# Three edits to a hybrid decoder layer kernel: a wider group of down tiles at a block's end, the order of the GLU's columns, and an early product taken from x without its 1/rms

## The chip, the cores and the metric

One core of a Trainium2 chip runs the whole layer as one program. The metric is the device time of one execution in microseconds (us). TensorE (PE, with its weight loads as PEld), VectorE (DVE), ScalarE (ACT), GpSimd (POOL) and SyncE (SP, which issues most DMAs) each work through a queue of their own, in order, and wait for each other by semaphores.

## The reference, cut to what matters

`norm(a)` is a / rms(a) times a gain; L = 2064 positions (16 meta tokens and 2048 tokens), 1024 features, 2816 hidden features in the MLP.

```python
h = concat(meta, x)                                   # 2064 x 1024
hn = norm(h)
b_gate, c_gate, v, u = split(hn @ w_in, 4)            # 512 columns each
conv_out = b_gate * causal_dwconv(c_gate * v)         # width 3
y = s5_scan(u) + d * u                                # 32 groups, 64 complex states each
g = gelu(y)
ssm_out = g * sigmoid(g @ w_glu)                      # the half-GLU, 512 x 512
h = h + concat(norm(conv_out), norm(ssm_out)) @ w_out
hn = norm(h)
up = causal_dwconv(hn @ w_up) + bias                  # 2 x 2816 columns
h = h + (silu(up[:, :2816]) * up[:, 2816:]) @ w_down
out = norm(h)[16:]
```

## The kernel before, in words

**Numbers.** Everything is float32. A product is made of two fp32r parts of each operand: a high part (`h_..`, `wh_..`, `ah`) that ACT rounds (L248) and a low part (`l_..`, `wl_..`, `al`) that DVE subtracts (L109). Three matmuls stand for one: high by high (L138), low by high (L139), high by low (L142). Features lie on the 128 partitions in k tiles, positions along the free axis.

**Positions.** The 2064 positions are cut into six pieces q of 344, and two pieces make one of three blocks b of 688 (in the MLP the first block has 672 and the others 688). A feature tile in PSUM or SBUF that holds a block has 128 x 688 elements, and one matmul takes 344 of them (336 in the first MLP block).

**Part one, projections.** `u_block(b)` (L877) makes the 512 columns of u of a block in four units of 8 k tiles x 2 pieces x 3 matmuls, and `conv_block(b)` (L896) the twelve units of v, c_gate and b_gate. The order written out is: u of block 0, conv of block 0, u of block 2 (early, L987), u of block 1, conv of block 1, conv of block 2. In the trace x of piece q is `x_c`, its scaled form `t_c`, its parts `h_c` and `l_c`, and the names in the program carry q: c4 and c5 are the two pieces of block 2. The 1/rms of a piece is made by squares (`sq_c`, L164), sums (DVE), a product with ones on PE (`st_c`, L188), a small scaling (`sv_c`), a power on POOL (L199), a diagonal (`dg_c`, L203), a product that spreads it (`sb_c`, L208), and a copy (`rs_c`, L213). For block 0, `raw_x` (L378) splits x times the gain straight into parts (ACT L389, DVE L390), and the 1/rms, kept in one buffer for two pieces (`rs0`, L373), is multiplied into what PE gives (`ut`, `vs`, `tc`, `tp`). For all other pieces `prep_x` (L348) multiplies the 1/rms into x first (`t_c`, 8 instructions at L241) and splits that; so c4 and c5 are scaled for the early u, and later loaded and scaled again for the conv of block 2. The steps of such preparations are generators that are stepped between the units (`after_unit`, L856); `late` holds last halves back until a unit has taken its place.

**Part two, GLU and output projection.** gelu(y) comes back from memory as `gt`, with 8 interleaved rows j of 258 columns per feature tile, so that position = 8 c + j. `prep_glu` (L1016) splits it (`gh` on ACT, `gl` on DVE) into position order: it reads rows j one after another in runs of 43 and writes with a step of 8 elements (`tokens`, L1007). `glu_block` (L1072) makes the product `pg`, the sigmoid `sg`, and multiplies it into `gt` in place. `prep_ssm` (L1026) squares `gt` (`sq_ms`), scales it (`t_ms`, contiguous) and splits it into position order (`h_ms`, `l_ms`). `mc` names the same steps for the conv half.

**Part three, MLP.** For each block, `up` (L1457) makes pairs of up tiles (`xy`, `z`), the conv and SiLU, and the split result `ah`, `al`; the 22 hidden tiles are in chunks of 4, 4, 4, 3, 3 and 4. `down` (L1499) multiplies a chunk into the 8 output tiles m. A list of groups of m says how many output tiles are open together: in a group every tile does all k but the chunk's last first, and then all do the last k, which is the one that is ready last. Before the last chunk a group holds two tiles (`first_pair`, L1535), at the end of blocks 0 and 1 three (L1555: the third in two tiles of the `z` pool). In the last block the end is done by pieces c of 344 with first_pair for c = 0. Each finished tile is copied by ACT (`ev`, L1525 or L1528, three buffers) and added to `h_d` in memory by a DMA of POOL (L1529); in the last block DVE adds it to `acc` instead. PSUM has two `xy` buffers, two `z` buffers and two `aux` buffers here. `Feed` (L1234) loads and splits the weights in order.

The order within each queue is made by a scheduler when the program is built, by its own estimates, under the dependences; so an edit can shift instructions that it does not name.

Of the kernel before, what the change touches and what calls it, by code (L numbers as in the profile page):

```python
# [11 lines left out]
F32 = mybir.dt.float32  # L12
# [45 lines left out]
def layer_kernel(ctx, tc, xq, pk, w_in, w_glu, w_out, w_up, w_down, ssm_s, ssm_m, y):  # L58
# [52 lines left out]
    def mul(out, a, b):  # L111
        tt(out, a, b, ALU.mult)
# [260 lines left out]
    def rs_tile(name):  # L373
        return cp.tile([P, 2, QM], F32, tag="rsk", bufs=1, name=name)

    rs0 = rs_tile("rs0")[:, :, :QL]

    def raw_x(q, res):  # L378


        xs, out = [], []
        for i in range(2):
            xs += load_halves((xq[q, :, 4 * i : 4 * i + 4, :],), QL, f"c{q}{i}")
            yield
        for i, x in enumerate(xs):
            hi, lo = hl_tile(QL, f"h_c{q}_{i}"), hl_tile(QL, f"l_c{q}_{i}")
            for k in range(4):
                g = col(C_MIX + 4 * i + k)
                S.activation(hi[:, k, :], x[:, k, :], AF.Copy, scale=g)  # L389
                V.scalar_tensor_tensor(  # L390
                    out=lo[:, k, :], in0=x[:, k, :], scalar=g, in1=f32(hi[:, k, :]), op0=ALU.mult, op1=ALU.subtract
                )
            out.append((hi, lo))
            yield
        res.append(out)
        yield from inv_rms(xs, QL, f"c{q}", rs0[:, q, :])


    sgn = col(C_SGN)
# [456 lines left out]
    def after_unit(n=1, n_prep=1):  # L856
        if a1 is None:
            ssm.step(4)
            if not ssm.q:
                start_a1()  # L860
                prep.add(prep_x(4, hu, other=True), prep_x(5, hu, late=late))
        else:
            ssm.step(n)
            prep.step(n_prep)
# [12 lines left out]
    def u_block(b, hs, last=False):  # L877
        rhs = rhs_of(hs)
        for m in range(4):
            if last and m == 3:  # L880
                while len(late) < 2:
                    prep.step()
            ps = unit(rhs, f"pu_{b}_{m}", m == 0 or last and m == 3)
            ut = cvp.tile([P, NJ, 86], F32, tag="ut", bufs=2, name=f"ut_{b}_{m}")
            if last and m == 3:
                take_late(2)
            by_j = lambda a: a.rearrange("p c (x j) -> p c x j", j=NJ)
            out = ut.rearrange("p j (c x) -> p c x j", c=2)
            if b == 0:
                mul(out, by_j(ps[:, :, :QL]), by_j(rs0))  # L890
            else:
                S.activation(out, by_j(ps[:, :, :QL]), AF.Copy)
            dma(out=u_d[:, m, :, b * 86 : b * 86 + 86].rearrange("j p c -> p j c"), in_=ut)
            after_unit(n_prep=5 if last else 1)

    def conv_block(b, hs, late_after=False, n_prep=1):  # L896
        rhs = rhs_of(hs)

        for j in range(4):
            pv_ = unit(rhs, f"cv_{b}_{j}", False)  # L900
            vs = cvp.tile([P, B2], F32, tag="cs", bufs=3, name=f"vs_{b}_{j}")
            if b == 0:
                mul(two(vs), pv_[:, :, :QL], rs0)
            else:
                S.activation(two(vs), pv_[:, :, :QL], AF.Copy)
            after_unit(n_prep=n_prep)
            pc = unit(rhs, f"cc_{b}_{j}", False)
            cv = cvp.tile([P, B2 + 2], F32, tag="cvt", bufs=1, name=f"cvt_{b}_{j}")
            V.tensor_copy(cv[:, 0:2], halo[:, j, :])
            if b == 0:  # L910
                mul(two(vs), two(vs), rs0)
            tt(two(cv[:, 2:]), pc[:, :, :QL], two(vs), ALU.mult)
            V.tensor_copy(halo[:, j, :], cv[:, B2 : B2 + 2])
            tp = cvp.tile([P, B2], F32, tag="cs", bufs=3, name=f"tc_{b}_{j}")
            S.activation(tp, cv[:, 2:], AF.Copy, scale=col(C_CW + 8 + j))
            axpy(tp, cv[:, 1 : B2 + 1], col(C_CW + 4 + j), tp)
            axpy(tp, cv[:, 0:B2], col(C_CW + j), tp)
            if b == 0:
                mul(two(tp), two(tp), rs0)
            after_unit(n_prep=n_prep)  # L920
            if late_after and j == 3:
                while len(late) < 2:
                    prep.step()
            pb = unit(rhs, f"cb_{b}_{j}", j == 3)
# [42 lines left out]

    hc = [[] for _ in range(3)]
    hu, late = [], []
    first = [raw_x(q, hc[0]) for q in range(2)]  # L970
    next(first[0])
    stream.raw.append(load_weights(*stream.items.popleft()))
    next(first[0])
# [42 lines left out]
    def prep_glu(b, res, **kw):  # L1016
        for c in range(2):
            hi, lo = hl_tile(QL, f"gh_{b}_{c}", **kw), hl_tile(QL, f"gl_{b}_{c}", **kw)
            c0 = (2 * b + c) * 43
            src = gt[:, :, :, c0 : c0 + 43]  # L1020
            S.activation(tokens(hi), src, AF.Copy)
            tt(tokens(lo), src, f32(tokens(hi)), ALU.subtract)
            res.append(((hi, lo),))
            yield

# [46 lines left out]
    def glu_block(b):  # L1072
        until(hg[b])
        rhs = rhs_of(hg[b])
        for m in range(4):
            ps = mm_tile(f"pg_{b}_{m}")
            product([ps[:, c, :QL] for c in range(2)], stream.take(), rhs, 4, by_chunk=m == 0)
            sg = ev_tile(f"sg_{b}_{m}")
            S.activation(two(sg), ps[:, :, :QL], AF.Sigmoid)
# [334 lines left out]
    for b in range(3):  # L1414
# [84 lines left out]
        def down(ci, ms, cs=(0, 1), into=None):  # L1499
# [51 lines left out]
        if b < 2:  # L1551
            while "scaled" not in hf[b + 1]:
                prep.step()
            hf[b + 1]["go"] = True
            for ms in [(0, 1, 2)] + [(m,) for m in range(3, KD)]:  # L1555
                down(last, ms)
                prep.step(len(ms))
            prep.drain()
# [3 lines left out]
        else:  # L1562
# [109 lines left out]
```

## Time and profile before

| | |
|---|---|
| time of three runs | 2195.51, 2195.66 and 2199.68 us, median 2195.66 us |
| the profiled execution | 2199.4 us, its span 2197.6 us |
| TensorE clock granted over the span | 0.984 of full speed |
| instructions in the span | 33162 |

The profiled execution took 2199.4 us, with 1.8 us of it outside the span. Rows of a timeline give start, duration, engine, line, operation, output <- inputs, tile shapes and xcount, and in brackets the idle time of the engine before it and what ended it. Rows of groups give a count, the busy time and the mean ns of one instruction. Rows of windows give a stretch, its length, each engine's busy time, the granted TensorE clock (1.00 is full speed), the share of the DMA engines and GB/s. Rows of waits give an engine and line, what was waited for, the total in us, how often, and the longest.

### The profile page before, as it was taken

Reading aid. Unit: us, or ns where it says so; the run is one execution under the profiler, and the core shown is the slowest. Engines: PE = TensorE matmul, PEld = TensorE weight load, DVE = VectorE, ACT = ScalarE, POOL = GpSimd, SP = SyncE. Lnnn points to the kernel's source line nnn. Section 1 sums busy time; section 2 is a strip of 40 time slices with the busy share of each in tenths; the row PEclk is TensorE's granted clock in tenths of the full one; section 3 lists DMA queues with packets and bytes.
Section 4 is the critical chain, followed back from the end, with each engine's and each line's share of the span. In section 5 each row is a group of like instructions: output and inputs, shape, how many; then the busy total and the mean of one; then the engine's idle time right before and its main releaser. Section 6 shows DMA issues by size and latency. Waiting matters only on the chain.

```text
span 2197.6 us, 33162 instructions
## 1 busy us (share of the span) xinstructions
PE 2119.1 (96%) x13012; PEld 2057.7 (94%) x13012; DVE 1688.0 (77%) x2539; ACT 1097.5 (50%) x1651; POOL 153.2 (7%) x174
## 2 busy tenths in 40 slices
PE   8997999999899999999999999999999999999997
PEld 7997999998898999999999999999899999999996
DVE  8896498857866796886679878777768878767776
ACT  4135333236523365554556556555456556545555
POOL 0000000000000001101110010100111010110010
PEclk9998999999999999999999999999999999999999
DMA  7376544352475336635552554744554362654463
GB/s 246 104 219 169 142 144 146 116 169 74 144 232 187 100 98 158 157 90 122 133 127 76 144 119 122 184 103 130 147 136 109 103 166 82 163 118 99 98 168 118
DMA packets 170750, 300.29 MB, mean 137 GB/s; under 512 B 32416, under 2 KB 104800, under 8 KB 170464
## 3 DMA queue, kind: packets, MB, share of 16 engines
q1 hardware_dynamic: 149856, 246.41, 36.3%
q0 software_dynamic: 19584, 47.52, 13.0%
q10 hardware_dynamic: 1152, 4.23, 0.5%
q8 instruction: 102, 1.67, 0.3%
q14 instruction: 56, 0.46, 0.1%
HBM read 214.29 MB, written 83.82 MB: 136 GB/s over the span
## 4 chain that ended last, share of the span: by engine, by line
PE 60%; issue 8%; DVE 5%; ACT 3%; DMA 3%; POOL 1%; SPq 0%; POOLq 0%; DVEq 0%; ACTq 0%
PE xy L1427 9%; PE xy L1429 8%; PE xy L1428 8%; PE dn L138 6%; PE dn L139 6%; PE dn L142 6%; PE pz L1429 3%; PE pz L1427 3%; PE pz L1428 3%; PE po L138 2%; PE po L142 2%; PE po L139 1%; DMA v_b<-h_d 1%; DMA gt<-g_d 1%; ACT h_ms L1038 1%
## 5 line engine op out<-in xcount | busy, mean ns | idle before, releaser
L109 DVE TENSOR_TENSOR wl_up<-wr_up,wh_up 128x1024 fp32r<-128x1024 f32 x198 | 241.8, 1222 | 140.7 <-ACT wh_up L248 138.5
L138 PE MATMUL dn<-ah,wh_dn 128*128 128x344 f32 (+1 forms) x1024 | 327.8, 324 | 11.4 <-ACT ah L248 8.8
L139 PE MATMUL dn<-al,wh_dn 128*128 128x344 f32 (+1 forms) x1024 | 325.5, 321 | 0.4 <-DVE al L109 0.3
L248 ACT ACTIVATE wh_up<-wr_up 128x1024 fp32r<-128x1024 f32 x198 | 209.6, 1059 | 230.8 <-PE dn L139 56.4
L1427 PE MATMUL xy<-h_t,wh_up 128*128 128x344 f32 (+1 forms) x792 | 262.8, 332 | 0.0
L1429 PE MATMUL xy<-h_t,wl_up 128*128 128x344 f32 (+1 forms) x792 | 253.4, 320 | 0.0
L1428 PE MATMUL xy<-l_t,wh_up 128*128 128x344 f32 (+1 forms) x792 | 252.7, 319 | 0.0
L142 PE MATMUL dn<-ah,wl_dn 128*128 128x344 f32 (+1 forms) x1024 | 248.1, 321 | 0.0
L138 PEld LDWEIGHTS dn<-ah,wh_dn 128*128 128x128 f32 x1024 | 193.2, 189 | 17.1 <-ACT ah L248 9.7
L1529 POOL DMA_DIRECT2D h_d<-ev x136 | 118.3, 870 | 1261.8 <-ACT ev L1525 1251.4
L139 PEld LDWEIGHTS dn<-al,wh_dn 128*128 128x128 f32 x1024 | 194.2, 190 | 2.0 <-DVE al L109 1.2
L1427 PE MATMUL xy<-h_b,wh_up 128*128 128x344 f32 (+1 forms) x528 | 175.6, 334 | 6.1 <-ACT ev L1525 4.6
L142 PEld LDWEIGHTS dn<-ah,wl_dn 128*128 128x128 f32 x1024 | 178.4, 190 | 0.0
L1428 PE MATMUL xy<-l_b,wh_up 128*128 128x344 f32 (+1 forms) x528 | 169.0, 320 | 0.0
L1429 PE MATMUL xy<-h_b,wl_up 128*128 128x344 f32 (+1 forms) x528 | 167.6, 320 | 0.0
L1427 PEld LDWEIGHTS xy<-h_t,wh_up 128*128 128x128 f32 x792 | 149.2, 188 | 17.1 <-ACT z L1472 11.1
L248 ACT ACTIVATE wh_dn<-wr_dn 128x512 fp32r<-128x512 f32 (+1 forms) x144 | 85.5, 594 | 133.6 <-issue 56.7
L1428 PEld LDWEIGHTS xy<-l_t,wh_up 128*128 128x128 f32 x792 | 149.9, 189 | 0.0
L1429 PEld LDWEIGHTS xy<-h_t,wl_up 128*128 128x128 f32 x792 | 149.6, 189 | 0.0
L115 DVE SCALAR_TENSOR_TENSOR g<-z,pv,g 128x688 f32<-128x688 f32 (+1 forms) x132 | 122.3, 926 | 23.7 <-ACT g L1432 22.9
L115 DVE SCALAR_TENSOR_TENSOR v<-z,pneg,v 128x688 f32<-128x688 f32 (+1 forms) x132 | 122.4, 927 | 10.3 <-ACT v L1432 9.0
L109 DVE TENSOR_TENSOR wl_dn<-wr_dn,wh_dn 128x512 fp32r<-128x512 f32 (+1 forms) x144 | 92.3, 644 | 45.6 <-ACT wh_dn L248 44.9
(413 smaller groups left out, 5358.3 us busy)
## 6 DMA issues: line engine op xcount, KB each, us to landing
wr_up<-in_w_up SPq DMA_DIRECT2D x132, 512.0 KB, 5.0
h_d<-ev POOLq DMA_DIRECT2D x88, 344.0 KB, 6.6
wr_dn<-in_w_down SPq DMA_DIRECT2D x96, 256.0 KB, 2.6
wr_cw<-in_w_in SPq DMA_DIRECT2D x36, 512.0 KB, 4.6
h_d<-ev POOLq DMA_DIRECT2D x48, 336.0 KB, 6.7
x_c<-in_xq SPq DMA_DIRECT2D x16, 688.0 KB, 6.4
wr_dn<-in_w_down SPq DMA_DIRECT2D x48, 192.0 KB, 2.3
xr<-in_xq SPq DMA_DIRECT2D x24, 344.0 KB, 3.7
```

The costliest lines, as they stand in the source:

```text
L109: V.tensor_tensor(out, a, b, op=op)
L115: V.scalar_tensor_tensor(out=out, in0=a, scalar=s, in1=b, op0=ALU.mult, op1=ALU.add)
L138: T.matmul(ps[c], hi[:, k, :], xh, start=k == 0, stop=False)
L139: T.matmul(ps[c], hi[:, k, :], xl, start=False, stop=False)
L142: T.matmul(ps[c], lo[:, k, :], xh, start=False, stop=k == nk - 1)
L248: S.activation(hi, t, AF.Copy)
L1038: S.activation(tokens(hi), t, AF.Copy)
L1427: T.matmul(ps, hi[:, j, :], xh[:, j, :], start=start and j == 0, stop=False, **kw)
L1428: T.matmul(ps, hi[:, j, :], xl[:, j, :], start=False, stop=False, **kw)
L1429: T.matmul(ps, lo[:, j, :], xh[:, j, :], start=False, stop=j == 3, **kw)
L1529: G.dma_start(out=h_d[:, m, s0 : s0 + no], in_=ev, accum_op=ALU.add)
```

## The change

It has three parts, and each stands by itself.

1. **Down at a block's end.** In blocks 0 and 1 the first group of the last chunk holds four tiles in place of three, and the fourth lies in two `aux` tiles. In block 2 the first group of piece c = 0 holds four tiles in place of two; the third and fourth lie in the `z` pool.
2. **GLU.** `gh` and `gl` keep the order of `gt` (8 rows j of 43) instead of position order, so that input and output are read and written in runs of 43. The product is over features, so its columns come out in the same order; `sg` is then read contiguous, and `gt` times `sg` runs over 43 at a time.
3. **Early u of block 2.** x of c4 is loaded right after u of block 0, and c4 and c5 go through `raw_x` in the place of `prep_x`: their parts are made from x times the gain, and their 1/rms (`rs_2`, in the one buffer that `rs_0` had) is multiplied into `ut` by DVE where ACT copied it. The later pass over c4 and c5, for the conv of block 2, is as it was.

```diff
@@ raw_x
-    def raw_x(q, res):
+    def raw_x(q, res, b, other=False, late=None):
...
+        kw = dict(pool=xf2, tag="xhl2", bufs=4) if other else {}
...
-        for i, x in enumerate(xs):
-            hi, lo = hl_tile(QL, f"h_c{q}_{i}"), hl_tile(QL, f"l_c{q}_{i}")
+        def split_half(i, x):
+            hi, lo = hl_tile(QL, f"h_c{q}_{i}", **kw), hl_tile(QL, f"l_c{q}_{i}", **kw)
...
-        yield from inv_rms(xs, QL, f"c{q}", rs0[:, q, :])
+        for i, x in enumerate(xs):
+            if late is None:
+                split_half(i, x)
+            else:
+                late.append(lambda x=x, i=i: split_half(i, x))
+            yield
+        if b not in rs_of:
+            rs_of[b] = rs_tile(f"rs_{b}")[:, :, :QL]
+        yield from inv_rms(xs, QL, f"c{q}", rs_of[b][:, q % 2, :])
@@ after_unit
-                prep.add(prep_x(4, hu, other=True), prep_x(5, hu, late=late))
+                prep.add(ahead[0], raw_x(5, hu, 2, late=late))
@@ u_block
-            if b == 0:
-                mul(out, by_j(ps[:, :, :QL]), by_j(rs0))
+            if b in rs_of:
+                mul(out, by_j(ps[:, :, :QL]), by_j(rs_of[b]))
@@ after u_block(0, hc[0])
+    ahead = [raw_x(4, hu, 2, other=True)]
+    next(ahead[0])
+    next(ahead[0])
@@ prep_glu
-            S.activation(tokens(hi), src, AF.Copy)
-            tt(tokens(lo), src, f32(tokens(hi)), ALU.subtract)
+            hj, lj = (a.rearrange("p k (j c) -> p k j c", j=NJ) for a in (hi, lo))
+            S.activation(hj, src, AF.Copy)
+            tt(lj, src, f32(hj), ALU.subtract)
@@ glu_block
-            g = gt[:, m, :, b * 86 : b * 86 + 86]
-            mul(g, g, tokens(sg))
+            g = gt[:, m, :, b * 86 : b * 86 + 86].rearrange("p j (c x) -> p c j x", c=2)
+            mul(g, g, two(sg).rearrange("p c (j x) -> p c j x", j=NJ))
@@ down
+                elif i < 2 + 2 // len(cs):
+                    ps = [ps_z.tile([P, 512], F32, tag="z", name=f"{name}_{c}")[:, :nn] for c in cs]
                 else:
-                    ps = [ps_z.tile([P, 512], F32, tag="z", name=f"{name}_{c}")[:, :nn] for c in cs]
+                    ps = [aux_tile(f"{name}_{c}")[:, :nn] for c in cs]
@@ the ends of blocks 0 and 1
-            for ms in [(0, 1, 2)] + [(m,) for m in range(3, KD)]:
+            for ms in [(0, 1, 2, 3)] + [(m,) for m in range(4, KD)]:
@@ the end of block 2
-                for ms in first_pair if c == 0 else [(m,) for m in range(KD)]:
+                for ms in [(0, 1, 2, 3)] + [(m,) for m in range(4, KD)] if c == 0 else [(m,) for m in range(KD)]:
```

The program still has 12752 instructions of PE and 2541 of DVE; ACT has 1671 in place of 1661; POOL's order is the same.

**PE at the end of block 0.** In `dn_0_5_m` the m is the output tile, and the next number its piece; `ah_0_20` and `ah_0_21` are the last two hidden tiles, of which 21 is the last to be ready. Before:

```order
L142 MATMUL dn_0_5_2_0_0_11213<-ah_0_20_11172,wl_dn0_5_2_11153 128x336
L142 MATMUL dn_0_5_2_0_1_11214<-ah_0_20_11172,wl_dn0_5_2_11153 128x336
L138 MATMUL dn_0_5_0_0_11211<-ah_0_21_11207,wh_dn0_5_0_11090 128x336
L138 MATMUL dn_0_5_1_0_11212<-ah_0_21_11207,wh_dn0_5_1_11129 128x336
L138 MATMUL dn_0_5_2_0_0_11213<-ah_0_21_11207,wh_dn0_5_2_11152 128x336
L138 MATMUL dn_0_5_2_0_1_11214<-ah_0_21_11207,wh_dn0_5_2_11152 128x336
```

And in the changed kernel:

```order
L142 MATMUL dn_0_5_3_0_0_11218<-ah_0_20_11175,wl_dn0_5_3_11200 128x336
L142 MATMUL dn_0_5_3_0_1_11219<-ah_0_20_11175,wl_dn0_5_3_11200 128x336
L138 MATMUL dn_0_5_0_0_11214<-ah_0_21_11210,wh_dn0_5_0_11093 128x336
L138 MATMUL dn_0_5_1_0_11215<-ah_0_21_11210,wh_dn0_5_1_11132 128x336
L138 MATMUL dn_0_5_2_0_0_11216<-ah_0_21_11210,wh_dn0_5_2_11155 128x336
L138 MATMUL dn_0_5_2_0_1_11217<-ah_0_21_11210,wh_dn0_5_2_11155 128x336
L138 MATMUL dn_0_5_3_0_0_11218<-ah_0_21_11210,wh_dn0_5_3_11199 128x336
L138 MATMUL dn_0_5_3_0_1_11219<-ah_0_21_11210,wh_dn0_5_3_11199 128x336
```

Three k tiles of output tile 3, 18 matmuls, now stand ahead of the first matmul that reads `ah_0_21`.

**ACT at the same place**, where it reads the finished tiles out (`ev`) and rounds weights (`wh_dn`). Before:

```order
L1528 ACTIVATE ev_0_5_2_11311<-dn_0_5_2_0_1_11214 128x336
L248 ACTIVATE h_b21_1_11443<-v_b21_1_10602 128x4x344
L248 ACTIVATE wh_dn0_5_7_11354<-wr_dn0_5_7_11291 128x512
L1525 ACTIVATE ev_0_5_3_11360<-dn_0_5_3_0_11329 128x672
L248 ACTIVATE h_t4_1_11364<-v_b11_1_10599 128x4x344
L248 ACTIVATE wh_up1_0_0_11393<-wr_up1_0_0_11300 128x1024
L1525 ACTIVATE ev_0_5_4_11402<-dn_0_5_4_0_11368 128x672
```

And in the changed kernel:

```order
L1547 ACTIVATE ev_0_5_2_11340<-dn_0_5_2_0_1_11217 128x336
L248 ACTIVATE h_b21_1_11448<-v_b21_1_10605 128x4x344
L1547 ACTIVATE ev_0_5_3_11350<-dn_0_5_3_0_0_11218 128x336
L248 ACTIVATE wh_dn0_5_7_11344<-wr_dn0_5_7_11320 128x512
L1547 ACTIVATE ev_0_5_3_11350<-dn_0_5_3_0_1_11219 128x336
L248 ACTIVATE h_t4_1_11369<-v_b11_1_10602 128x4x344
L248 ACTIVATE wh_up1_0_0_11398<-wr_up1_0_0_11329 128x1024
L1544 ACTIVATE ev_0_5_4_11407<-dn_0_5_4_0_11373 128x672
```

Tile 3 is read out in two halves, one on either side of the rounding of the weights of tile 7; the readout of tile 4 still stands behind that rounding.

**PE in the early u of block 2**, where `pu_2_m` is unit m, `c4_0` the first half of the k tiles of c4, and `c5_1` the second half of c5. Before, after the last matmul of unit 0 on c4:

```order
L138 MATMUL pu_2_1_1881<-h_c4_0_1510,wh_u21_1740 128x344
L139 MATMUL pu_2_1_1881<-l_c4_0_1511,wh_u21_1740 128x344
L138 MATMUL pu_2_2_1969<-h_c4_0_1510,wh_u22_1805 128x344
L139 MATMUL pu_2_2_1969<-l_c4_0_1511,wh_u22_1805 128x344
L188 MATMUL st_c5_1648<-ones_80,sq_c5_0_1584 115x1 x3
L208 MATMUL sb_c5_1660<-dg_c5_1656,ones_80 128x344
L138 MATMUL pu_2_0_1804<-h_c5_0_1794,wh_u20_1665 128x344
```

In the changed kernel unit 0 goes on with all of c5_0 (12 matmuls, of which the last two are shown) and then:

```order
L139 MATMUL pu_2_0_1807<-l_c5_0_1786,wh_u20_1666 128x344
L142 MATMUL pu_2_0_1807<-h_c5_0_1785,wl_u20_1667 128x344
L138 MATMUL pu_2_1_1884<-h_c4_0_1417,wh_u21_1731 128x344
L138 MATMUL pu_2_0_1807<-h_c5_1_1795,wh_u20_1666 128x344
L139 MATMUL pu_2_1_1884<-l_c4_0_1418,wh_u21_1731 128x344
L138 MATMUL pu_2_1_1884<-h_c5_0_1785,wh_u21_1731 128x344
```

The matmuls of c5 no longer stand behind `st_c5` and `sb_c5`, which come 26 and 42 rows later; one product of c5_1 stands early, ahead of most of unit 1.

**DVE a little later**, where c2 and c3, the pieces of block 1, are prepared. Before:

```order
L109 TENSOR_TENSOR l_c2_1_1962<-t_c2_1_1956,h_c2_1_1961 128x4x344
L109 TENSOR_TENSOR wl_u12_2128<-wr_u12_1886,wh_u12_2127 128x1024
L109 TENSOR_TENSOR sq_c3_0_2027<-sq_c3_0_2027,sq_c3_1_2029 128x4x344
L109 TENSOR_TENSOR sq_c3_0_2027<-sq_c3_0_2027 128x2x344
L109 TENSOR_TENSOR sq_c3_0_2027<-sq_c3_0_2027 128x344
```

And in the changed kernel:

```order
L109 TENSOR_TENSOR l_c2_1_1965<-t_c2_1_1959,h_c2_1_1964 128x4x344
L109 TENSOR_TENSOR ut_2_2_2027<-pu_2_2_1972,rs_2_1437 128x86x8
L109 TENSOR_TENSOR wl_u12_2131<-wr_u12_1889,wh_u12_2130 128x1024
L109 TENSOR_TENSOR sq_c3_0_2030<-sq_c3_0_2030,sq_c3_1_2032 128x4x344
L109 TENSOR_TENSOR ut_2_3_2118<-pu_2_3_2063,rs_2_1437 128x86x8
L109 TENSOR_TENSOR sq_c3_0_2030<-sq_c3_0_2030 128x2x344
L109 TENSOR_TENSOR wl_u13_2193<-wr_u13_1977,wh_u13_2192 128x1024
L109 TENSOR_TENSOR sq_c3_0_2030<-sq_c3_0_2030 128x344
```

Two readouts of u and one weight split now stand between the steps of the sum of squares of c3.

More of the change, by code (lines that the diff above doesn't have):

```diff
@@ L374, in rs_tile @@
         return cp.tile([P, 2, QM], F32, tag="rsk", bufs=1, name=name)
-    rs0 = rs_tile("rs0")[:, :, :QL]
-    def raw_x(q, res):
+    rs_of = {}
+    def raw_x(q, res, b, other=False, late=None):
         xs, out = [], []
+        kw = dict(pool=xf2, tag="xhl2", bufs=4) if other else {}
         for i in range(2):
@@ L384, in raw_x @@
             yield
-        for i, x in enumerate(xs):
-            hi, lo = hl_tile(QL, f"h_c{q}_{i}"), hl_tile(QL, f"l_c{q}_{i}")
+        if other:
+            kw["pool"] = xf2
+        def split_half(i, x):
+            hi, lo = hl_tile(QL, f"h_c{q}_{i}", **kw), hl_tile(QL, f"l_c{q}_{i}", **kw)
             for k in range(4):
@@ L393, in raw_x @@
             out.append((hi, lo))
+            if i == 1:
+                res.append(out)
+        for i, x in enumerate(xs):
[3 more added lines that the diff above has]
+                late.append(lambda x=x, i=i: split_half(i, x))
             yield
-        res.append(out)
-        yield from inv_rms(xs, QL, f"c{q}", rs0[:, q, :])
+        if b not in rs_of:
+            rs_of[b] = rs_tile(f"rs_{b}")[:, :, :QL]
+        yield from inv_rms(xs, QL, f"c{q}", rs_of[b][:, q % 2, :])
     sgn = col(C_SGN)
@@ L902, in conv_block @@
             if b == 0:
-                mul(two(vs), pv_[:, :, :QL], rs0)
+                mul(two(vs), pv_[:, :, :QL], rs_of[0])
             else:
@@ L910, in conv_block @@
             if b == 0:
-                mul(two(vs), two(vs), rs0)
+                mul(two(vs), two(vs), rs_of[0])
             tt(two(cv[:, 2:]), pc[:, :, :QL], two(vs), ALU.mult)
@@ L918, in conv_block @@
             if b == 0:
-                mul(two(tp), two(tp), rs0)
+                mul(two(tp), two(tp), rs_of[0])
             after_unit(n_prep=n_prep)
@@ L969, in layer_kernel @@
     hu, late = [], []
-    first = [raw_x(q, hc[0]) for q in range(2)]
+    first = [raw_x(q, hc[0], 0) for q in range(2)]
     next(first[0])
```

## Prediction, made before the result

> **What bounds the kernel now.** I read the page's busy times first, then the waits of TensorE, then windows and timelines around the places where the diff acts. The page's row:
>
> ```profile
> PE 2119.1 (96%) x13012; PEld 2057.7 (94%) x13012; DVE 1688.0 (77%) x2539; ACT 1097.5 (50%) x1651; POOL 153.2 (7%) x174
> ```
>
> TensorE is busy for 2119.1 of 2197.6 us. The change takes no matmul away, so it can only gain from the 78.5 us in which PE stands, and from matmuls that run at a low clock after such a stand. The waits that the three parts touch (total, times, longest):
>
> ```profile
> PE dn L138 <- ACT ah L248: 8.8, 3, 3.4
> PE st_c L188 <- DVE sq_c L109: 4.4, 2, 3.3
> PE pu L138 <- ACT h_c L248: 4.4, 2, 4.0
> PE sb_c L208 <- DVE dg_c L203: 3.6, 2, 2.9
> PE st_ms L188 <- DVE sq_ms L109: 2.5, 2, 1.8
> PE pg L142 <- DVE wl_g L109: 2.3, 1, 2.3
> ```
>
> They add up to 26.0 us. The first row is the three block ends, the next three the early u, the last two the GLU. What a stand costs beyond itself is in the granted clock, the column before the last two:
>
> ```profile
> 161.00:176.00 15.00, 3.99 (x15) 2.16 (x13) 11.95 (x23) 3.16 (x3) 1.20 (x1) 0.67 0.72 229
> 176.00:180.00 4.00, 3.91 (x14) 3.91 (x15) 2.58 (x3) 2.71 (x2) 0.00 (x0) 0.54 0.53 178
> 215.00:219.00 4.00, 3.88 (x24) 3.88 (x25) 1.58 (x2) 2.72 (x3) 0.00 (x0) 1.00 0.86 304
> 530.00:542.00 12.00, 10.21 (x50) 10.06 (x49) 8.65 (x15) 5.26 (x7) 2.03 (x2) 0.72 0.16 45
> ```
>
> Right after the long stand at 161, 14 matmuls fill 4 us at clock 0.54; at clock 1.00, 24 fill as much. So a matmul goes on in 0.287 us cold and 0.157 warm, and each cold one costs 0.13. A cold stretch is some 12 of them, about 1.6 us.
>
> **Part 1: the GLU.** Groups of like instructions (count, busy and mean ns):
>
> ```profile
> L1021 ACT ACTIVATE gh<-gt 128x1376 fp32r<-128x1376 f32 x6 | 17.6, 2938 | 3.3 <-DMA gt<-g_d 3.3
> L109 DVE TENSOR_TENSOR gl<-gt,gh 128x1376 fp32r<-128x1376 f32 x6 | 17.5, 2914 | 10.6 <-ACT gh L1021 10.5
> L109 DVE TENSOR_TENSOR gt<-gt,sg 128x688 f32<-128x688 f32 x12 | 17.8, 1486 | 2.7 <-ACT sg L1079 2.7
> L164 ACT ACTIVATE sq_ms<-gt 128x1376 f32<-128x1376 f32 x6 | 8.1, 1367 | 4.8 <-DVE gt L109 3.5 <-DVE l_mc L109 1.2
> L109 DVE TENSOR_TENSOR l_mc<-t_mc,h_mc 128x1376 fp32r<-128x1376 f32 x6 | 9.4, 1590 | 0.1
> 603.27 0.86 DVE L109 TENSOR_TENSOR xr<-kp,xr 128x688 f32<-128x688 f32 x1
> ```
>
> `sq_ms` reads the same runs of 43 of the same `gt` and writes without a step: 1367 ns, against 2938 for `gh`. So I price the new `gh` at 1.37 us (1.57 less), `gl` at 1.59 by the contiguous split `l_mc` (1.32 less), and `gt` times `sg` at 0.86 by the contiguous `xr` (0.62 less). The bounds are these and the old durations, since runs of 43 on DVE with two inputs have no row. What it does for PE:
>
> ```profile
> 497.62 2.90 ACT L1021 ACTIVATE gh<-gt 128x1376 fp32r<-128x1376 f32 x1 [3.34 <-DMA gt<-g_d]
> 507.51 0.65 PE L142 MATMUL pg<-gh,wl_g 128*128 128x344 f32 x1 [2.26 <-DVE wl_g L109]
> 529.10 2.63 ACT L164 ACTIVATE sq_ms<-gt 128x1376 f32<-128x1376 f32 x2 [3.49 <-DVE gt L109]
> 534.60 1.20 PE L188 MATMUL st_ms<-ones,sq_ms 128*115 128x1 f32 x6 [1.79 <-DVE sq_ms L109]
> 564.04 1.29 PE L188 MATMUL st_mc<-ones,sq_mc 128*115 128x1 f32 x6 [4.87 <-DVE sq_mc L109]
> ```
>
> At 507.51 PE has waited 2.26, since 505.25, for a weight split that stands on DVE behind two `gl`. With the new prices the two `gh` and the split weights are through by about 503, before PE comes. The wait goes, and 12 cold matmuls with it (1.5): **3.8**. At 534.60 PE waits 1.79 for `sq_ms`, which ACT begins at 529.10 after four of DVE's `gt`; DVE has been working without a break. Six `gl` and four `gt` less are 7.9 and 2.5, so DVE is no longer last, and `sq_ms` follows the sigmoid instead. PE's wait goes, and with it the low clock of 530 to 542 (0.72 on average, 19 long matmuls x 0.13, and slower small ones, some 3.3): **5.1**. The stretch to 564 is DVE's again: two `gt` fewer at 0.62, **1.2**. The wait of 4.87 stays, as `l_ms` and `sq_mc` are untouched. Sum **10.1**; with old durations on one side it is 5, and 12 if the 1.2 comes more than once.
>
> **Part 2: the early u of block 2.**
>
> ```profile
> 161.16 0.32 PE L139 MATMUL pu<-l_c,wh_u 128*128 128x344 f32 x1
> 176.09 0.65 PE L139 MATMUL pu<-l_c,wh_u 128*128 128x344 f32 x1 [0.85 <-DVE l_c L109]
> 189.33 0.74 PE L208 MATMUL sb_c<-dg_c,ones 115*128 115x344 f32 x2
> 192.01 3.99 DVE L241 SCALAR_TENSOR_TENSOR t_c<-x_c,pv,rs_c 128x344 f32<-128x344 f32 x8 [0.48 <-ACT rs_c L213]
> 215.12 0.43 PE L139 MATMUL pu<-l_c,wh_u 128*128 128x344 f32 x1 [1.34 <-DVE l_c L109]
> 7.38 2.04 DVE L390 SCALAR_TENSOR_TENSOR l_c<-x_c,pv,h_c 128x344 fp32r<-128x344 f32 x4 [5.90 <-ACT h_c L389]
> 24.99 1.99 ACT L389 ACTIVATE h_c<-x_c,pv 128x344 fp32r<-128x344 f32 x4
> DMA to landing us min/median/max: 4.1/6.4/9.1
> L109 DVE TENSOR_TENSOR ut<-pu,rs x4: 1450/1494/1534, 37.4 to 48.9; 128x688 f32<-128x688 f32 x4
> ```
>
> From 161.3 PE stands for `sq_c`, `dg_c`, `h_c` and `l_c` of c5 (3.3, 2.9, 4.0 and 0.85). Split without its 1/rms, a half of c5 costs 2.0 on ACT and 2.0 on DVE (the two rows of four), and can begin when its x lands. So PE goes on with what had been waiting: 105 matmuls of u at 0.157 (16.4), the small products of c5 and c2 (1.9), and small gaps, put at 2.0. Taken from 160.7, where unit 0 has used up c4, `sb_c` of c2 comes at 181.0 instead of 189.33, and I take 8.3 for `t_c` as well. From `t_c` at 192.01 to PE's restart at 215.12 the old chain took 23.1 us: c2 is split, c3 is summed, scaled and split. Into it come two `ut` on DVE (2 x 1.49, where ACT copied), and a weight split of 1.2 that stood behind; of these 4.2 DVE's idle stretches there take up about 2.7. So the restart is 8.3 - 1.5 = 6.8 earlier. The wait before it was 1.34 and left the clock warm (1.00 in 215 to 219); it gets longer now, and I take 1.3 off for a cold stretch: **5.5**. Upper bound: no cold stretch and all of 8.3, and with the 1.6 saved at 176, 10. Lower bound: 0, when c3's chain, which starts no earlier than its own loads and PE's `st_c`, eats it all.
>
> **Part 3: the group of four.**
>
> ```profile
> 1196.53 1.21 PE L138 MATMUL dn<-ah,wh_dn 128*128 128x336 f32 x4 [2.87 <-ACT ah L248]
> 1206.08 0.63 ACT L248 ACTIVATE wh_dn<-wr_dn 128x512 fp32r<-128x512 f32 x1 [2.15 <-DMA wr_dn<-in_w_down]
> 1210.02 0.73 ACT L1525 ACTIVATE ev<-dn 128x672 f32<-128x672 f32 x1 [0.50 <-DMA h_d<-ev]
> 1212.09 0.32 PE L138 MATMUL dn<-ah,wh_dn 128*128 128x336 f32 x1
> 1680.38 0.90 PE L138 MATMUL dn<-ah,wh_dn 128*128 128x344 f32 x4 [2.60 <-ACT ah L248]
> 1694.05 0.75 ACT L1525 ACTIVATE ev<-dn 128x688 f32<-128x688 f32 x1 [0.28 <-DMA h_d<-ev]
> 1696.62 0.32 PE L138 MATMUL dn<-ah,wh_dn 128*128 128x344 f32 x1
> 2151.70 0.59 PE L138 MATMUL dn<-ah,wh_dn 128*128 128x344 f32 x2 [3.37 <-ACT ah L248]
> 2166.66 0.52 DVE L109 TENSOR_TENSOR acc<-dn,acc 128x344 f32<-128x344 f32 x1 [0.27 <-PE dn L142]
> ```
>
> *Blocks 0 and 1.* A fourth tile brings 3 k x 2 pieces x 3 = 18 matmuls ahead of `ah`, 2.8 us; the waits are 2.87 and 2.60. They and their cold stretch (1.6) go: some 4.5 each by the time tile 6 would begin (1212.09 and 1696.62 before, so 1207.6 and 1692.1). But tile 6 takes the `xy` buffer of tile 4, which `ev` of tile 4 empties; that one waits, at 1210.02 and 1694.05, for the DMA that adds tile 1 to memory, as there are three `ev` buffers. ACT has the rounding of tile 7's weights ahead of it as well (2.15 of waiting for its DMA). Tile 1 is read out only a little sooner. So tile 6 begins when this `ev` ends: 1210.1 and 1694.2 by half a us less than now, a gain of 2.0 and 2.4. PE stands some 2.3 before it and gets cold, 1.6 each. That leaves 0.4 + 0.8, about **1.1** (both rounded down). Bounds: 9 with no such wait, and 0.
>
> *The last block.* Two more tiles bring 2 x 9 matmuls, 2.8 us, against 3.37. A wait of about half a us is left, but the next stretch is bound by DVE's rows, so the cold clock costs the same as now: last sum of c = 0 at 2163.9 in place of 2166.66, **2.8** (2 to 4.5).
>
> **Sum.** 10.1 + 5.5 + 1.1 + 2.8 = 19.5 us. The profiled execution of 2199.4 would take 2179.9; from the median of the three runs, 2195.66, it is **2176.2**.
>
> **The rivals.** *R1: short waits leave the clock warm.* Then the new waits at tile 6 (2 x 1.6) and before the restart (1.3), 4.5 in all, cost nothing beyond themselves: 2171.7. For it: 1.34 at 215.12 left it warm. Against it: 1.79 at 534.60 is followed by 0.72. [...]
>
> *R2: the early u gives nothing.* c3's chain, or the load of the second half of c5, ends as late as now: 2176.2 + 5.5 = 2181.7. For it: c3's loads and PE's `st_c` of c3 aren't in the diff, and PE idles behind them either way.
>
> *R3: runs of 43 are not as cheap on DVE with two inputs.* The second stall and the DVE stretch stay, the GLU gives 5: 2181.3. Against it: `sq_ms`.
>
> *R4, the other side: x of c5's second half lands late.* One product of `h_c5_1` stands in PE's order right behind c5_0, ahead of the rest of unit 1, and PE is in order. It is due at 160.7 + 13 x 0.157 = 162.7; the load is issued when the half before it on SP's queue and its buffer are through, near 156, and should land at 161. From 162.7 each us later is a us of PE. After 15 us of delay the sum is within 4.4 us of no change (0.2%, about what a measurement of this kernel can tell), and from 24 on it is slower: over 2200.1, 2201 say. The longest of 16 loads of x took 9.1.
>
> *R5: the group of four covers nothing.* `aux` holds also the products of the next block's 1/rms, and a tile that waits for it would stand in front of the group: parts 1.1 and 2.8 go, 2180.1.
>
> **How the numbers follow.** Forecast 0.46, R1 0.12, R2 0.20, R3 0.07, R5 0.06: all faster by over 0.2%, 0.91. R4 has 0.09: 0.05 within 0.2%, and 0.04 slower. The range: from 2176.2 down by 7.9 (block ends at 9) and 1.9 (GLU at 12), 2166.4, and up by R2 and R3 together, 2186.8: 2166 to 2187. Outside it is R4 and little else.
>
> **What would show it.** Right: `gh` near 1.4 us and `gl` near 1.6; no wait of `pg` for `wl_g`; no `sq_c`, `dg_c` and `h_c` waits before the early u; `dn` for `ah` near 0 at the two block ends with a new wait of `dn` for `ev` of 2 to 2.5 there, and 0.5 at the tail. Wrong: `gl` above 2.2, `t_c` of c2 later than 188, a PE wait on `h_c` of over 3 us near 163, or no wait at tile 6, when the time is under 2170.

## The result, and the profile after

| | |
|---|---|
| changed kernel, four runs | 2176.65, 2177.22, 2183.6 and 2185.31 us, median 2180.41 us |
| kernel before, beside it | median 2195.59 us |
| ratio | 0.993, interval 0.9901 to 0.9958 |
| the profiled execution | 2183.6 us, its span 2181.8 us (before 2199.4 and 2197.6) |
| the same kernel in a later comparison, five runs | 2176.61 to 2186.42 us, median 2179.32; ratio 0.9912, interval 0.9896 to 0.9927 |

So it is 15 to 20 us faster: 0.7% in the first comparison, 0.9% in the second. The first row of the changed kernel's page, and those of TensorE's waits that the change touches (total, times, longest):

```profile
PE 2116.5 (97%) x13012; PEld 2056.3 (94%) x13012; DVE 1670.2 (77%) x2539; ACT 1086.5 (50%) x1661; POOL 153.6 (7%) x174
```

```profile
PE dn L138 <- ACT ev L1544: 7.3, 2, 4.2
PE st_mc L188 <- DVE sq_mc L109: 4.3, 1, 4.3
PE pu L138 <- ACT h_c L248: 4.0, 1, 4.0
PE dn L138 <- DVE acc L109: 3.5, 2, 2.3
PE sb_c L208 <- DVE dg_c L203: 2.7, 3, 2.1
PE dn L138 <- ACT ah L248: 1.6, 1, 1.6
PE st_c L188 <- DVE sq_c L109: 1.5, 2, 1.1
```

The two rows of the GLU are gone. `ah` has fallen from 8.8 to 1.6, and `dn` for `ev`, 1.2 before, is now 7.3 in two waits: those that the prediction put before tile 6.

To see where the time went I cut each trace at steps that every kernel has. The table gives the microseconds between the starts of these steps; "adds out" is a kernel told of below that leaves out part of the result. The steps are the products with ones for a 1/rms: of x (`st_c`), of the MLP's input (`st_f`) and of the last norm (`st_y`, `st_last`).

| stretch | before | changed | GLU only | early u only | down only | ends back | tile 4 by DVE | adds out |
|---|---|---|---|---|---|---|---|---|
| start to the last `st_c` | 331.5 | 329.8 | 333.7 | 328.3 | 333.7 | 326.1 | 328.5 | 326.6 |
| to the first `st_f` (GLU, output projection) | 367.2 | 354.3 | 355.3 | 364.8 | 367.1 | 354.1 | 354.4 | 354.3 |
| to the next norm's `st_f` in block 0 | 134.7 | 135.4 | 133.6 | 132.2 | 132.2 | 135.2 | 135.3 | 132.1 |
| to the last `st_f` (holds the end of block 0) | 707.8 | 707.3 | 706.7 | 706.5 | 706.8 | 706.9 | 703.7 | 701.9 |
| to the last `st_y` (holds the end of block 1) | 325.3 | 325.2 | 327.4 | 325.4 | 325.9 | 325.3 | 325.2 | 319.1 |
| to the first `st_last` (tail) | 301.8 | 299.8 | 302.1 | 301.7 | 299.6 | 299.4 | 300.1 | 299.2 |
| to the end | 29.3 | 30.0 | 30.0 | 29.3 | 29.9 | 29.9 | 30.0 | 29.7 |

Between the profiled executions the GLU gave 12.9 us, the tail 2.0 (of which 0.7 goes again in the last row), the block ends 0.6 together, and the first stretch only 1.7. In block 1's stretch there is one more wait, which no edit names: near 1550 PE waits for ACT's readout, 4.60 us before and 2.69 in the changed kernel and in "adds out", 4.30 to 4.64 in the other columns. These 1.9 us hide that the wait of `dn` near 1680 grew from 2.60 to 4.24.

**The first stretch** holds the early u and, before it, something that no edit touches. Near 85 us PE makes 32 small products (`kps`), and the clock is low from there on. Windows of the kernel before, then of the changed one:

```profile
85.00:105.00 20.00, 20.00 (x118) 19.82 (x119) 9.78 (x24) 4.03 (x8) 0.00 (x0) 0.74 0.37 112
```

```profile
85.00:105.00 20.00, 19.64 (x95) 19.46 (x96) 8.07 (x16) 3.24 (x6) 0.00 (x0) 0.57 0.28 86
```

The granted clock (third column from the end) is 0.74 in the one and 0.57 in the other. That is 3.4 us of full speed lost (0.17 x 20), in the changed kernel's disfavour. The kernel "ends back", whose instructions are the changed kernel's in the same order up to 1170 us, has 0.74 again in its row:

```profile
85.00:105.00 20.00, 19.86 (x118) 19.66 (x119) 10.71 (x34) 3.51 (x7) 0.00 (x0) 0.74 0.40 124
```

So the program does not set it, and without this loss the first stretch is 5.1 us shorter than before. Nine traces in all have this program up to the GLU (two of the changed kernel, and those of seven more runs told of below), and the clock was low near 85 us for three, four or five windows of 3.4 us, by the clock records of the traces (five are 17.07 us, from 86.44 to 103.51 in the changed kernel's first trace). Their first stretch goes with that number: 325.8 to 326.6 us with three, 327.8 to 328.6 with four, 329.8 and 330.2 with five. The kernel before has three windows (10.24 us, from 87.56 to 97.80) and 331.5.

### The profile page after: what moved, and what is told of

Same layout as the page of the kernel before. It is cut to its first block, busy times and chain, and to the rows that moved or that the text cites. A ratio compares the mean times of both kernels' runs of the same rounds, so it can differ in the third digit from the quotient of the medians.

```text
span 2181.8 us, 33169 instructions
## 1 busy us (share of the span) xinstructions
PE 2116.5 (97%) x13012; PEld 2056.3 (94%) x13012; DVE 1670.2 (77%) x2539; ACT 1086.5 (50%) x1661; POOL 153.6 (7%) x174
```

## The experiments

**The parts alone.** Three kernels have one part each on the kernel before; their edit is the part of the diff above. A fourth, "ends back", is the changed kernel with

```diff
-            for ms in [(0, 1, 2, 3)] + [(m,) for m in range(4, KD)]:
+            for ms in [(0, 1, 2)] + [(m,) for m in range(3, KD)]:
```

Expected of the GLU alone:

> Only part 2 of the change (GLU columns in the order of gt) on the kernel before. Theory 'the parts are independent': the stretch from the first GLU product to the 1/rms of the first MLP block gets 12.8 us shorter, as between the two traces (473.3 to 684.1 against 475.1 to 698.7), and so does the time; gh 1.37, gl 1.59, gt times sg 0.87 us. Rival 'the prediction's own sum': 10.1 us, and the other 2.7 come from the other parts arriving differently.

Measured: 2186.11 us against 2196.8, ratio 0.9946 (0.9933 to 0.9958), so 11.9 us (9.2 to 14.7); in the trace the stretch of the GLU is 11.9 us shorter. The theory's 12.8 and the prediction's 10.1 both lie in the interval. The stretches of the GLU in the table tell more: 364.8 to 367.2 without the edit and 354.1 to 355.3 with it, 11.9 between their means. The costs are the priced ones; groups of the changed kernel:

```profile
L109 DVE TENSOR_TENSOR gt<-gt,sg 128x688 f32<-128x688 f32 x12 | 10.4, 870 | 4.8 <-ACT sg L1096 4.8
L109 DVE TENSOR_TENSOR gl<-gt,gh 128x1376 fp32r<-128x1376 f32 x6 | 9.5, 1588 | 8.6 <-ACT gh L1038 8.6
L1038 ACT ACTIVATE gh<-gt 128x1376 fp32r<-128x1376 f32 x6 | 8.2, 1373 | 3.4 <-DMA gt<-g_d 3.4
```

Each fell from 1486, 2914 and 2938 ns to within 10 ns of its price.

Expected of the early u alone:

> Only part 3 of the change (x of block 2 without its 1/rms for the early u). Theory 'chance of the clock': the units before the early u are no slower than before; the 2.7 us that the changed kernel lost between 84 and 117 us, where the clock stood at half speed for longer, come and go from run to run; the restart after c3 lies some 6.8 us earlier against the same point, a cold stretch follows, and the time falls by 4.5 us. Rival 'the edit costs there': the stretch from 84 to 117 us is 2.7 us longer in this kernel too, and the time falls by 1.8 us.

Measured: 2190.18 against 2196.8, ratio 0.9966 (0.9953 to 0.9979), 7.5 us (4.6 to 10.3). The trace's first stretch, with the low clock near 85 us reckoned at the same 3 windows of 3.4 us for all (1.7 us off for each further one), is 326.6; the three kernels without the edit have 330.3 to 332.0, where 3.4 us are taken off "GLU only" for a low clock near 208 us. That makes 3.7 to 5.4 us, some 5. "The edit costs there" falls, as its 1.8 us lie outside the interval; "chance of the clock" stands in what it says of the windows (four here, as in "down only", which hasn't the edit), though its 4.5 us lie just outside too.

Expected of the group of four alone:

> Only part 1 of the change (the group of four at the ends of blocks 0 and 1 and in the last block). Theory 'the wait moves': at both block ends the wait of dn for ah goes and a wait of dn for ev of 3 to 4 us takes its place, with no gain beyond 0.5 us in the two together; the tail gains 2.1 us, the time falls by 2 to 2.5 us. Rival 'the group covers': 2 us or more at each block end, 6 us in all.

Measured: 2196.95 against 2196.8, ratio 0.9995 (0.9985 to 1.0005): 1 us, between 3 faster and 1 slower, where 2 to 2.5 were expected. The waits at the block ends are those foretold; from its timeline:

```profile
1209.15 0.49 PE L138 MATMUL dn<-ah,wh_dn 128*128 128x336 f32 x1 [3.54 <-ACT ev L1527]
1694.20 0.66 PE L138 MATMUL dn<-ah,wh_dn 128*128 128x344 f32 x1 [3.34 <-ACT ev L1527]
```

2.87 and 2.60 for `ah` have become 3.54 and 3.34 for `ev`. The tail gained 2.2 (301.8 to 299.6), of which 0.6 goes again by the end (29.3 to 29.9).

Expected of "ends back":

> The changed kernel with the groups of three put back at the ends of blocks 0 and 1; the tail keeps its four. Theory 'the wait moves': the same time as the changed kernel within 0.5 us, 13 to 15 us below the kernel before. Rival 'the group covers': 4 us slower than the changed kernel.

Measured: 2176.91, ratio 0.9903 (0.9888 to 0.9918), no slower than the changed kernel (0.9912 and 0.993), and further below the kernel before than expected. "The group covers" falls: the group of four at the two block ends is worth nothing that can be measured (706.9 and 325.3 us without it, 707.3 and 325.2 with it).

**What tile 6 waits for.** The prediction said an `ev` buffer, free only when tile 1's DMA has landed. In the changed kernel's trace ACT's timeline and the chain of waits at that place say otherwise:

```profile
1193.98 1.06 ACT L248 ACTIVATE wh_up<-wr_up 128x1024 fp32r<-128x1024 f32 x1 [1.73 <-DMA wr_up<-in_w_up]
1194.94 0.71 ACT L1544 ACTIVATE ev<-dn 128x672 f32<-128x672 f32 x1
```

```profile
1186.33 7.56 DMA wr_up<-in_w_up
```

A buffer's DMA is not what `ev` of tile 4 waits for last. It stands in ACT's queue behind the rounding of the next block's first weights, and their load takes 7.56 us. Two edits tell buffer and queue apart, and a third kernel has both. The first takes two of the z buffers for the readouts of tiles 3 and 4:

```diff
-                    ev = ev2_tile(f"ev_{b}_{ci}_{m}")[:, :no]
+                    ev = (z_tile if ci == last and m in (3, 4) else ev2_tile)(f"ev_{b}_{ci}_{m}")[:, :no]
```

The second has DVE read tile 4 out:

```diff
-                        S.activation(two(ev), whole[m], AF.Copy)
+                        if ci == last and m == 4:
+                            V.tensor_copy(two(ev), whole[m])
+                        else:
+                            S.activation(two(ev), whole[m], AF.Copy)
```

Expected of the first:

> The changed kernel, with the readouts of tiles 3 and 4 at a block's end in two of the z buffers, which nothing else uses then, so that tile 4's readout needs no free ev buffer. Theory 'buffers' (the prediction's: tile 4's readout waits for tile 1's DMA): the wait of dn for ev at the two block ends, 3.1 and 4.2 us, falls below 1 us, and the time by 4 us or more with the cold stretches. Theory 'queue' (ACT works in order, and the rounding of the next block's first wh_up, which waits for its load, stands ahead of tile 4's readout): the wait stays at 3 to 4 us and the time as it is.

Measured: 2180.29, ratio 0.9914 (0.99 to 0.9929), against 0.9912 for the changed kernel beside it. The waits stayed:

```profile
1189.15 0.65 PE L138 MATMUL dn<-ah,wh_dn 128*128 128x336 f32 x1 [3.68 <-ACT ev L1544]
1675.18 0.43 PE L138 MATMUL dn<-ah,wh_dn 128*128 128x344 f32 x1 [3.23 <-ACT ev L1544]
```

"Buffers" has fallen. Expected of the second:

> The changed kernel, with tile 4 at a block's end read out by DVE instead of ACT, into the same ev buffers. Theory 'buffers': the wait of dn for tile 4's readout stays, as tile 1's DMA still has to land first: tile 6 begins at most 0.7 us sooner. Theory 'queue': the wait falls to below 1 us, as DVE has nothing there that waits for a load, and the time falls by 4 us or more.

Measured: 2176.82, ratio 0.9897 (0.9881 to 0.9913). The waits are shorter and not gone; and the clock stays full after them (windows of the same kernel):

```profile
1192.32 0.39 PE L138 MATMUL dn<-ah,wh_dn 128*128 128x336 f32 x1 [1.44 <-DVE ev L1545]
1677.13 0.39 PE L138 MATMUL dn<-ah,wh_dn 128*128 128x344 f32 x1 [2.49 <-DVE ev L1545]
```

```profile
1190.00:1200.00 10.00, 8.56 (x55) 8.19 (x54) 7.74 (x9) 4.92 (x7) 2.27 (x3) 1.00 1.07 267
1675.00:1685.00 10.00, 7.87 (x50) 7.90 (x51) 8.10 (x9) 4.34 (x6) 2.39 (x3) 1.00 1.00 237
```

"Queue" is right for some 1.7 us of each wait, and missed in "below 1 us": with ACT out of the way, 1.4 to 2.5 us are left. These are the buffer's, as DVE's timeline shows; its readout waits for the DMA that adds an earlier tile to memory:

```profile
1191.31 0.86 DVE L1545 COPY ev<-dn 128x672 f32<-128x672 f32 x1 [1.54 <-DMA h_d<-ev]
1676.11 0.88 DVE L1545 COPY ev<-dn 128x688 f32<-128x688 f32 x1 [2.87 <-DMA h_d<-ev]
```

So the buffer is a limit too, but it comes free sooner than the queue. By the table block 0's stretch is 3.6 us shorter than the changed kernel's and block 1's no shorter (325.2): the wait near 1550 is 4.63 here and is followed by two low windows in place of one. Expected of both edits:

> The changed kernel with both edits: tiles 3 and 4 read out into z buffers, tile 4 by DVE. Both theories: no wait of dn for ev before tile 6 of over 1 us, 2 x (2 to 3 us and most of a cold stretch) less, 4 to 8 us below the changed kernel, if no later wait at the start of the next block (its first wh_up is rounded no sooner than now) takes it back. If one does, the time is within 1 us of the changed kernel and a wait of xy for wh_up shows.

Measured: 2180.44, ratio 0.9916 (0.9903 to 0.993), no gain. No wait of `dn` for `ev` is left at either end, but PE now waits for the same weights itself:

```profile
1192.10 0.65 PE L1444 MATMUL pz<-h_t,wh_up 128*128 128x344 f32 x1 [3.57 <-ACT wh_up L248]
1192.83 0.53 PE L138 MATMUL dn<-ah,wh_dn 128*128 128x336 f32 x1
1677.49 0.43 PE L1444 MATMUL pz<-h_t,wh_up 128*128 128x344 f32 x1 [2.82 <-ACT wh_up L248]
```

The down tiles are not done by then. The scheduler has put two matmuls of the next block ahead of the last two tiles, whose 48 matmuls begin at 1192.83; PE takes them in that order and waits 3.57 us in front of them. So this run shows that the two limits together hold `dn`, and not what both edits would give in the old order of PE, where these 48 matmuls, over 7 us of work, could stand ahead of that wait. The last of this group is the changed kernel beside the three:

> The changed kernel once more, beside the next three. The stages are as in its first trace, but for the stretch of small matmuls near 85 to 117 us, whose low clock lasted 3 to 5 windows of 3.4 us in six traces so far; if that length is chance, this trace may show another one, and the time lies between 2176 and 2185 us, in the middle near 2179. If the length belongs to the kernel, 5 windows again, and the median is 2183 us or more.

It had 5 windows again in its trace, with a time of 2186.42 for that execution; the other four runs took 2176.61 to 2181.0, and the median is 2179.32. The median speaks for chance, this trace by itself does not; the nine traces above, three to five windows with one program, settle it.

**Why the weights are late.** A kernel without the adds to memory of tiles 0 to 6 at the two ends, which so leaves out part of the result:

```diff
-                    G.dma_start(out=h_d[:, m, s0 : s0 + no], in_=ev, accum_op=ALU.add)
+                    if ci != last or m == KD - 1:
+                        G.dma_start(out=h_d[:, m, s0 : s0 + no], in_=ev, accum_op=ALU.add)
```

> The changed kernel without the DMAs that add tiles 0 to 6 of the last chunk to memory at the ends of blocks 0 and 1 (that part of the result is left out; the readouts stay). Theory 'contention': the load of the next block's first weights, for which ACT's rounding of wh_up waits ahead of tile 4's readout, is slow because the DMA engines are full (share 1.06 to 1.10 in 1190 to 1200); without the adds it lands at least 2 us sooner, the wait of dn for ev falls below 1.5 us at both block ends, and each end gets 2 us or more shorter. Rival 'issue': the load is only issued when a buffer of raw weights comes free, near 1186 at the earliest, and lands no sooner than before by 1 us; the wait stays over 2.5 us.

Measured: 2168.22, ratio 0.9856 (0.9839 to 0.9873); PE has no wait over 0.15 us at either end. The loads of `wr_up` near the end of block 0, in the changed kernel and then in this one:

```profile
DMA to landing us min/median/max: 3.8/7.6/9.3
```

```profile
DMA to landing us min/median/max: 3.5/3.5/4.6
```

And the share of the DMA engines (the column before the last) when the adds are there:

```profile
1190.00:1195.00 5.00, 2.63 (x18) 2.35 (x16) 2.28 (x2) 3.24 (x5) 0.86 (x1) 1.00 1.06 291
1195.00:1200.00 5.00, 4.29 (x18) 4.29 (x19) 4.37 (x6) 2.44 (x4) 1.73 (x2) 0.66 1.10 264
1675.00:1680.00 5.00, 0.86 (x6) 0.57 (x4) 2.15 (x2) 2.23 (x3) 0.50 (x1) 1.00 1.07 307
```

The load is issued 5.2 us after `ah` is done in both kernels (1186.33 against 1181.12, and 1179.33 against 1174.10), so "issue" falls: the load takes longer while the adds are under way (a share of 1.06 to 1.10). Each block end is 5 to 6 us shorter without them (table; the wait near 1550 is alike in the two, 2.69 and 2.70). The adds hold both limits, the load of the weights and the buffer: what PE gains by a fourth tile it waits out behind these DMAs. How the 5 to 6 us divide between the two isn't shown.

**Inside the GLU.** The sigmoid read in steps of 8 again:

```diff
-            mul(g, g, two(sg).rearrange("p c (j x) -> p c j x", j=NJ))
+            mul(g, g, two(sg).rearrange("p c (x j) -> p c j x", j=NJ))
```

> The changed kernel with the sigmoid read in steps of 8 again in gt times sg (its columns then stand in the wrong order, so the GLU's result is not the reference's), with gh and gl as changed. It divides the GLU's 11.8 us. If gt times sg goes back to 1.4 to 1.5 us, the prediction's terms say that DVE is still not last at the first two stalls (six gl give 7.9 us, four gt 2.5): the two waits of pg and st_ms stay below 1 us, the stretch before st_mc gets 1.2 us longer, and the time by 1 to 2 us. Rival: the gain is mostly in gt times sg, and the time goes up by 5 us or more.

Measured: 2183.27, ratio 0.9929 (0.9911 to 0.9946), where the changed kernel has 0.9912: some 3.7 us dearer, the intervals overlap. In the trace the GLU's stretch is 357.6 instead of 354.3. The group is back at its old price,

```profile
L109 DVE TENSOR_TENSOR gt<-gt,sg 128x688 f32<-128x688 f32 x12 | 18.0, 1503 | 4.0 <-ACT sg L1096 4.0
```

and no wait of `pg` or of the first `st_ms` is back. So `gh` and `gl` alone end the two stalls, as the terms had it; the other part, `gt` times `sg`, is worth 3.3 in the trace and not 1.2.

**The load ahead, and tile 4 by DVE once more.** The first takes out the two `next(ahead[0])`.

> The changed kernel without the load of x of c4 ahead of its place: c4 and c5 are loaded where the kernel before loaded them. Theory 'the scaling was the wait': the time is the changed kernel's within 1 us, and the early u shows no wait on h_c of c4 or c5. Rival 'the load was the wait': a PE wait of 2 us or more on h_c before 165 us, and a time up by as much.

Measured: 2179.79, ratio 0.9911 (0.9894 to 0.9927), the changed kernel's own, and no wait on `h_c` before 165 us. So what the early u gains comes from leaving the 1/rms out, the only other part of that edit.

> The changed kernel with tile 4 at a block's end read out by DVE, once more. If its gain over the changed kernel is real, 2 to 4 us as on the other chip (ratio to the kernel before 0.9897 against 0.9912), the ratio is again below 0.991 and the waits of dn for ev are again 1 to 2.5 us; if it was chance in the clock, the ratio lies at 0.992 or above.

Measured: 2177.48, ratio 0.9894 (0.9878 to 0.991), with waits of 1.28 and 1.97. Both times this kernel was the fastest of its group with all of the work in it; its ratios of 0.9897 and 0.9894 against the changed kernel's 0.9912 make 3 to 4 us. Its interval meets that of the changed kernel, and "ends back" had 0.9903, so it is likely, and not shown, to be better. That it beats the kernel before is shown.

## Why the prediction was right, point by point

It gave 2176.2 us in 2166 to 2187, and 19.5 us of gain; measured were 2180.4 with a gain of 15.2 in the first comparison, and 2179.3 with 20.4 in the second. That the sum came this close is in part luck: the GLU gave some 2 us more than its term, and the other three terms together some 2 to 3 less.

*GLU, 10.1.* Right in mechanism, some 2 us too small (11.9). Both stalls went as described, and in the window that had the clock at 0.72 it is now full:

```profile
530.00:542.00 12.00, 12.00 (x73) 11.19 (x73) 9.59 (x21) 7.75 (x9) 1.17 (x1) 1.00 0.07 24
```

The mis-sized term is "two `gt` fewer at 0.62, 1.2": the step of `gt` times `sg` was worth 3.3. One reading is a little off: 24 matmuls in the 3.88 us that PE was busy are 0.162 us each; the 0.157 is the distance of matmuls in the timelines.

*Early u, 5.5.* Right: some 5 by the stage, 7.5 (4.6 to 10.3) by the runs. From DVE's and PE's timelines of the changed kernel:

```profile
184.12 0.82 PE L208 MATMUL sb_c<-dg_c,ones 115*128 115x344 f32 x2 [0.28 <-DVE dg_c L203]
185.92 3.99 DVE L241 SCALAR_TENSOR_TENSOR t_c<-x_c,pv,rs_c 128x344 f32<-128x344 f32 x8
200.60 0.76 PE L188 MATMUL st_c<-ones,sq_c 128*115 128x1 f32 x6 [1.15 <-DVE sq_c L109]
203.43 1.52 PE L208 MATMUL sb_c<-dg_c,ones 115*128 115x344 f32 x2 [2.07 <-DVE dg_c L203]
208.96 1.23 PE L138 MATMUL pu<-h_c,wh_u 128*128 128x344 f32 x3 [4.01 <-ACT h_c L248]
211.02 0.65 PE L139 MATMUL pu<-l_c,wh_u 128*128 128x344 f32 x1 [0.84 <-DVE l_c L109]
```

Less the 3.4 us lost near 85 us, `sb_c` comes at 180.7 (181.0 foretold) and the restart at 207.6, 7.5 before 215.12 (6.8 foretold). The waits moved from c5 to c3, 8.1 us of them in 200 to 211, and the cold stretch after them came: the window 200 to 215 has

```profile
200.00:215.00 15.00, 7.48 (x25) 5.95 (x26) 9.56 (x17) 5.88 (x5) 0.85 (x1) 0.58 0.54 146
```

*Block ends, 1.1.* Right that the gain is nearly eaten by a wait before tile 6, wrong in what it waits for. The step "that one waits for the DMA that adds tile 1 to memory, as there are three `ev` buffers" failed: with two buffers more the wait stayed at 3.2 to 3.7. The load of the next block's first weights, slowed by the adds, is last; through ACT's queue it holds tile 4's readout. The buffer comes second: it holds 1.3 to 2.5 us of the wait when DVE reads tile 4 out. The waits are 3.1 and 4.2 where 2 to 2.5 were foretold, and the gain is nothing instead of 1.1. The sum had ACT "with the rounding of tile 7's weights ahead of it", and overlooked the row behind that one in the order, the rounding of `wh_up`.

*Tail, 2.8.* Right in direction, too large. The table's row of the tail gives 1.7 to 2.6, but the last row takes some of it back: from the last `st_y` to the end it is 331.0 to 332.1 us without the edit and 328.9 to 330.1 with it, 1.9 between the means. The term overlooked a wait of 0.90 on `z` just before the 3.37. The 18 matmuls cover that first and then leave 1.63 where 0.5 was foretold, and a longer wait follows for the buffers that DVE empties. Before, and then two rows of the changed kernel:

```profile
2146.65 0.43 PE L138 MATMUL dn<-ah,wh_dn 128*128 128x344 f32 x1 [0.90 <-DVE z L109]
```

```profile
2137.31 0.90 PE L138 MATMUL dn<-ah,wh_dn 128*128 128x344 f32 x4 [1.63 <-ACT ah L248]
2149.86 0.40 PE L138 MATMUL dn<-ah,wh_dn_0b 128*128 128x344 f32 x1 [2.25 <-DVE acc L109]
```

*The rivals.* R2 (no gain in the early u), R3 (runs of 43 dear on DVE) and R4 (late x) did not come; `h_c5_1`'s load was in time. Nor did R5: no wait for `aux` shows, the group of four covers its wait for `ah`, and that it gives nothing at two of its three places has the other reason told above. R1 did not come at the places that it names: the waits before tile 6 were 3.08 and 4.24, longer than foretold, and the clock fell after both (0.66 in 1195 to 1200 and in 1680 to 1685), as it did before the restart. Whether a wait of some 2 us leaves the clock warm stays open: 2.49 at 1677 in "tile 4 by DVE" left it at 1.00.

## What to carry to other kernels

Here a write or read in steps of 8 float32 elements cost ACT and DVE 1.7 to 2.1 times as much as in runs of 43, and the analogous row without steps in the same trace gave the new price to within 10 ns. When an edit lets one engine arrive earlier at the end of a block, ask which load the next block begins with, and what else the DMA engines move at that moment: here the time gained was waited out behind that load. Read every row between a readout and its predecessor in its queue, not only the first one that waits.

## What the runs showed of the hardware

The 32 products of 128 x 128 by 16 columns (two matmul instructions each in the trace) take 12.87 us in the changed kernel and 10.57 in the kernel before, by their timelines:

```profile
85.36 12.87 PE L616 MATMUL kps<-w,mats 128*128 128x16 f32 x64 [1.00 <-DVE w L611]
```

```profile
83.93 10.57 PE L603 MATMUL kps<-w,mats 128*128 128x16 f32 x64 [1.01 <-DVE w L598]
```

PE is never idle there, and yet the clock is at half for part of this stretch and beyond it, into full-size matmuls, for 3 to 5 windows of 3.4 us. In the clock records of the kernel before and of the changed kernel, the 19 low stretches that ended before the trace did were of 3.41, 6.83, 10.24, 13.65 or 17.07 us, one to five times 3.41. In the clock records of all fourteen traces the number near 85 us goes with how soon the clock falls. It falls 1.0 to 4.4 us after the first of these products, and the sooner it falls, the longer it stays low: five windows after 1.0 and 1.1 us (two traces), four after 2.0 to 3.0 (seven), three after 3.4 to 4.4 (five). In the changed kernel above it falls after 1.1 us and is full again at 103.51, 5.3 us after the last of these products ends; in the kernel before it falls after 3.6 us and is full again at 97.80, 3.3 us after their end. What sets the moment of the fall isn't shown. A window more costs some 2 us (first stretch, above); that is at most 4 of the 10 us between the runs of the changed kernel, and where the rest is lost isn't shown.

A short wait did not settle here what the clock did. Near 207 us PE waits about as long in the kernel before (1.11 and 0.70) as in "GLU only" (1.29 and 0.41), in the same program; the windows of the two:

```profile
205.00:215.00 10.00, 7.31 (x42) 6.30 (x42) 7.72 (x16) 5.53 (x5) 0.85 (x1) 1.00 0.54 126
```

```profile
205.00:215.00 10.00, 8.29 (x34) 7.13 (x33) 6.99 (x15) 4.01 (x4) 0.85 (x1) 0.67 0.56 122
```

1.00 in the one, 0.67 in the other; what made the difference isn't shown. And 1.79 us of waiting, ended at 534.60 in the kernel before, with products of one column on both sides of it, had a low stretch of 6.83 us behind it (534.70 to 541.53; 0.72 in 530 to 542).
